# Two consecutive rows of one expert on each partition: another cut of the expert loads in a mixture-of-experts block

## The chip, the core and the metric

The kernel runs on one core of one Trainium2 chip. The metric is the device time of one execution in microseconds; lower is better. The core has a matrix engine (TensorE: PE, and PEld for its weight loads), VectorE (DVE), ScalarE (ACT), GpSimd (POOL) and SyncE (SP), which here issues nearly all DMAs, and 16 DMA engines that share each load.

## What is computed

A block of a small language model for 256 tokens of 1024 features, all in float32: a recurrent mixer and an attention mixer, gated and projected, then a layer norm, then 32 experts in 4 groups of 8, each token sent to two experts of its best group, then a second layer norm. The part that the change touches is the experts:

```python
x = layer_norm(DN_ALPHA * h + mixed, ln1_g[l], ln1_b[l])
ffn = hier_moe(x, ...)
# in hier_moe, for the tokens xb of an expert e:
gate, up = jnp.split(xb @ w_gate_up[e], 2, axis=-1)      # w_gate_up[e]: 1024 x 1024
y = (jax.nn.silu(gate) * up) @ w_down[e]                 # w_down[e]: 512 x 1024
x = layer_norm(DN_ALPHA * x + ffn, ln2_g[l], ln2_b[l])
```

A product sums over the rows of the expert's matrix, so these rows may be taken in any order as long as the features of the tokens stand in the same one.

## The kernel before

The first part (lines 191 to 1007) computes the two mixers, the first norm and the routing. Its weights pass through four places of 8 KB a partition (`W_PL`), each loaded as 512 rows of 512 columns.

The second part (from line 1146) takes the experts in 8 quads of 4 (`NQ`). The 24 loads of a quad (`NEXP`) are 1 MB each, numbered `i = 24 q + r`: r = 0 to 15 hold w_gate_up, r = 16 to 23 w_down. `e_source` (L124) gives the source: the 128 rows of the chunk k of two experts, each partition getting one row (4 KB) of either. So loads 2k and 2k + 1 bring the chunk k of the quad's four experts. Loads go to places in the order of `E_PL` (24 places, one of which becomes the accumulator); a place is used again 23 loads later. `e_tile` (L181) issues the loads in order of their number, all on SP; some are issued far ahead, in the first part, as its own buffers come free. Loads 8, 10 and half of 25 are issued as halves (`e_halves`, L131) into other buffers. In the last quad the down loads are cut by columns instead (L151 to L166): 512 columns of all four experts (r = 16 to 19), then 256 (20, 21), then 128 (22, 23).

For each quad, `gather` (L887) makes `xg`: for each k, a matmul whose weights are the 128 normed features `hx[:, t, k * P:(k + 1) * P]` and whose moving operand places up to 32 tokens of each expert; ScalarE and VectorE apply the norm's gain and bias (`g1_cols`, `b1_cols`, from the rows that are loaded at L205 and transposed at L394). Then `by_expert` (L1137) issues, for k = 0 to 7 and each half j of the columns, four matmuls, one for each expert on its own 32 columns of the array; each shows as two instructions. `act_T` (L1041) applies the activation, transposes the 128 x 512 result in four pieces (L1048) and `by_expert` multiplies by the down weights, k = 0 to 3. `combine` (L1056) adds the weighted result to the accumulator within the next quad, after its k = 1; the gather for the next quad stands after k = 4. In the last quad, down products, combine and the norm's statistics follow each other by column slices (L1191 to L1228), and then come the closing norm and the stores. Behind a condition that this input doesn't meet stands `overflow` (L1098).

Of the kernel before, what the change touches and what calls it, by code (L numbers as in the profile page):

```python
# [16 lines left out]
ALU = mybir.AluOpType  # L17
# [3 lines left out]
P = 128  # L21
# [39 lines left out]
def kernel(ctx: ExitStack, tc: tile.TileContext, x, w_in, b_in, rows_in, relb, w_proj_a, w_proj_b,  # L61
# [56 lines left out]
    def e_place(i):  # L118
# [2 lines left out]
        n = len(E_PL) - 1  # L121
        return E_PL[i] if i < n else (E_PL[:N_ACC] + E_PL[N_ACC + 1:])[(i - n) % n]

    def e_source(i):  # L124

        q, r = divmod(i, NEXP)
        src, k = (w_gate_up[0], r // 2) if r < 16 else (w_down[0], (r - 16) // 2)
        e0 = 4 * q + 2 * (r % 2)
        return src[e0:e0 + 2, k * P:(k + 1) * P, :].rearrange("e p c -> p e c")

    def e_halves(i, halves, ns=(0, 1)):  # L131

        ts = e_tiles.setdefault(i, [None] * 2)
        for n in ns:
            nc.sync.dma_start(halves[n], e_source(i)[:, n])
            ts[n] = halves[n]

    def e_get(i):
        q, r = divmod(i, NEXP)
        if i == E_SPL:  # L140
            e_halves(i, [part(n, "e_half") for n in (1, 2)])
            return
        if i == E_PART:
            p = place(E_PL[-1], "e_t")
            e_halves(i, (part(3, "e_half"), p[0]))
            e_halves(E_NEXT, (p[1],), (0,))
            return
        t = place(e_place(i), "e_t")
        if i == E_NEXT:
            e_halves(i, (None, t[0]), (1,))  # L150
        elif q == NQ - 1 and 16 <= r < 20:  # L151

            t = t[2].rearrange("p (e c) -> p e c", e=4)
            r0 = (r - 16) * P
            nc.sync.dma_start(t, w_down[0, 4 * q:4 * q + 4, r0:r0 + P, 0:512].rearrange("e p c -> p e c"))
            e_tiles[i] = [t[:, e, :] for e in range(4)]
        elif q == NQ - 1 and r >= 20:

            nk, w = (2, 256) if r < 22 else (4, 128)
            c0, k0 = (512, 2 * (r - 20)) if r < 22 else (768 + 128 * (r - 22), 0)  # L160
            t = t[2].rearrange("p (k e c) -> p k e c", k=nk, e=4)
            for k in range(nk):
                r0 = (k0 + k) * P
                nc.sync.dma_start(t[:, k], w_down[0, 4 * q:4 * q + 4, r0:r0 + P, c0:c0 + w].rearrange(
                    "e p c -> p e c"))
            e_tiles[i] = [[t[:, k, e, :] for e in range(4)] for k in range(nk)]  # L166
        else:
            t = t[2].rearrange("p (e c) -> p e c", e=2)
            nc.sync.dma_start(t, e_source(i))  # L169
            e_tiles[i] = [t[:, e, :] for e in range(2)]  # L170

    e_next = [0]

# [9 lines left out]
            e_load()  # L183
        return e_tiles[i]

    def e_rows(i, j):

        return [w[:, j * 512:(j + 1) * 512] for n in range(2) for w in e_tile(i + n)]


    xs = place(XS, "xs")[2].rearrange("p (t d) -> p t d", t=NT)
# [8 lines left out]
    run(wl[0])  # L200
    x_load(512, 1024)
    run(wl[1])
    NR = 88
    rows = const.tile([NR, P], F32, name="rows")
    nc.sync.dma_start(rows, rows_in)  # L205
    run(w_load())
# [195 lines left out]
        return cols[:, 32 + c // P:32 + c // P + n]  # L402

    g1_cols, b1_cols, ng_cols = cols[:, 0:8], cols[:, 8:16], cols[:, 84:88]
    lnr = rows[0:32]
    nb_f = const.tile([P, HG], F32, name="nb_f")
    nc.vector.tensor_scalar(nb_f, bias_cols(C_F, HG), -1.0, None, op0=ALU.mult)
# [479 lines left out]
    def gather(pos_of, idx, tl, groups=(range(0, 4), range(4, 8))):  # L887

        oh, xg = tl["oh"], tl["xg"]
        n = idx.shape[-1]  # L890
        j = P // n
        banks = [big1("px") for g in groups]

        def pick(b, k, t):
            g = groups[b]
            dst = banks[b][:, (k - g[0]) * P:(k - g[0] + 1) * P]
            nc.tensor.matmul(dst, hx[:, t, k * P:(k + 1) * P], oh[:, t, :], start=(k == g[0] and t == 0),  # L897
                             stop=(k == g[-1] and t == 1), skip_group_check=True)
            return dst

        def rows_of(t):
            return nc.vector.tensor_tensor(v3(oh[:, t, :], n), pos_of(t)[:, :, None].to_broadcast([P, j, n]),
                                           idx[:, None, :].to_broadcast([P, j, n]), op=ALU.is_equal)

        rows_of(0)
        yield
        for b in (0, 1):
            for k in groups[b]:
                pick(b, k, 0)
        rows_of(1)  # L910
        for b, g in enumerate(groups):
            if b == 1:
                for c in range(2, len(groups)):
                    for k in groups[c]:
                        pick(c, k, 0)
            for k, pk in [(k, pick(b, k, 1)) for k in g]:
                if k % 2:
                    xg_put[:] = [nc.vector.tensor_scalar(xg[:, k, :], pk, g1_cols[:, k:k + 1], b1_cols[:, k:k + 1],  # L918
                                                         op0=ALU.mult, op1=ALU.add)]
                else:  # L920
                    nc.scalar.activation(xg[:, k, :], pk, AF.Identity, bias=b1_cols[:, k:k + 1],  # L921
                                         scale=g1_cols[:, k:k + 1])
            yield

    def places_of(q, tl, **kw):
# [115 lines left out]
    def act_T(gu):  # L1041
        sg = y_tile()[:, 0:512]
        nc.scalar.activation(sg, gu[:, 0, :], AF.Sigmoid)  # L1043
        nc.vector.tensor_tensor(sg, gu[:, 0, :], sg, op=ALU.mult)  # L1044
        nc.vector.tensor_tensor(sg, gu[:, 1, :], sg, op=ALU.mult)
        ph = big1("ph")
        for k in range(4):
            nc.tensor.transpose(ph[:, k * P:(k + 1) * P], sg[:, k * P:(k + 1) * P], ident)  # L1048
        nc.scalar.activation(h_tile()[:, 0:512], ph, AF.Copy)

    def y_out(py):
# [46 lines left out]
    def overflow():  # L1098
# [4 lines left out]
        with tc.If(cmx > CAP):  # L1103
            with tc.For_i(0, NE) as e:
                ce = nc.values_load(cnt[0:1, bass.ds(e, 1)], min_val=0, max_val=S)
                for g in range(2):
                    with tc.If(ce > CAP + g * P):
# [8 lines left out]
                        for k in range(KD):  # L1116
                            for j in range(2):
                                w = y_tile()[:, j * 512:(j + 1) * 512]
                                nc.gpsimd.dma_start(w, w_gate_up[0, bass.ds(e, 1), k * P:(k + 1) * P,
                                                               j * 512:(j + 1) * 512].rearrange("e p c -> p (e c)"))  # L1120
                                nc.tensor.matmul(gu[:, j, :], xg[:, k, :], w, start=(k == 0), stop=(k == KD - 1))
                        act_T(gu)
# [2 lines left out]
                        for k in range(4):  # L1125
                            for j in range(2):
                                w = xw[:, j * 512:(j + 1) * 512]
                                nc.gpsimd.dma_start(w, w_down[0, bass.ds(e, 1), k * P:(k + 1) * P,
                                                            j * 512:(j + 1) * 512].rearrange("e p c -> p (e c)"))
                                nc.tensor.matmul(py[:, j, :], hT_of(k), w, start=(k == 0), stop=(k == 3))  # L1130
                        y_out(py)
# [15 lines left out]
    for q in range(NQ):  # L1147
# [7 lines left out]
        for k in range(KD):  # L1155
# [5 lines left out]
                with tc.issue_after(ins):  # L1161
                    run(feed)
            for j in range(2):
                ins = by_expert(gu[:, j, :], tl["xg"][:, k, :], e_rows(n0 + 2 * k, j), k == 0, k == KD - 1,
                                pin=q == 0 and j == 0)
            if k == 1 and pending:
                combine(wT_of(q - 1))
# [17 lines left out]
        if q < NQ - 1:  # L1185
            for k in range(4):
                for j in range(2):
                    by_expert(py[:, j, :], hT_of(k), e_rows(n0 + 16 + 2 * k, j), k == 0, k == 3)
            y_out(py)
            pending = True  # L1190
        else:  # L1191
# [85 lines left out]
def _layout(i):  # L1277
# [1 line left out]
    def r(n):  # L1279
        return np.asarray(i[n]).reshape(-1, P)  # L1280

    i["rows"] = np.concatenate([r(n) for n in ("ln1_g", "ln1_b", "ln2_g", "ln2_b", "b_in", "lb_logits", "hg_norm_g")])
    rel = np.concatenate([np.asarray(i["rel_bias"]), np.ones((1, MH), np.float32)])
    i["relb"] = np.concatenate([rel, _bucket_rows()], axis=1)
    wg, we = np.asarray(i["w_group"])[0], np.asarray(i["w_expert"])[0]
# [20 lines left out]
```

## Time and profile before

| | |
|---|---|
| median of 3 runs | 670.04 us (669.97 to 670.57) |
| the profiled execution | 670.6 us, its span 669.0 us |
| PE busy, PEld busy | 555.9 us (83%), 311.9 us (47%) |
| DVE, ACT, POOL busy | 229.3 us, 162.2 us, 9.2 us |
| DMA | 238.48 MB, 356 GB/s over the span |
| mean granted TensorE clock | 0.944 |

The span runs from the first to the last instruction of the profiled execution. A busy engine need not be the one that sets the time: matmuls are pipelined and waits for a load can lie within them. The page divides the span into 40 slices and gives for each the busy share of the engines, the granted clock and what the DMA moved; the chain follows the work that ended last back through what released it.

### The profile page before, as it was taken

The numbers are of one execution on the slowest core, as the hardware profiler recorded it, in microseconds if no ns is written. First come the engines' busy times: TensorE is split into PE (matmuls) and PEld (weight loads), VectorE is DVE, ScalarE is ACT, GpSimd is POOL, SyncE is SP. The second block draws the span as 40 slices with busy tenths as digits, with TensorE's granted clock in tenths as the row PEclk, the third lists the DMA queues.
The fourth block names the chain that finished last, engine by engine and source line by source line (L and its number), as shares of the span: only waits on it lengthen the run. The fifth ranks groups of instructions, "written<-read, shape, count | busy, mean of one in ns | idle before, by whom it ended". The sixth has DMA issues, their size and how long they took to land.

```text
span 669.0 us, 9743 instructions
## 1 busy us (share of the span) xinstructions
PE 555.9 (83%) x4018; PEld 311.9 (47%) x4019; DVE 229.3 (34%) x531; ACT 162.2 (24%) x321; POOL 9.2 (1%) x32
## 2 busy tenths in 40 slices
PE   8999999999998989897666865786776778677686
PEld 8989899999987543323111311131121113123124
DVE  4698668866577314220010002010201010020027
ACT  5653568955553200101000100010001001001010
POOL 1000000000000000000000000000000000000000
PEclk9999999999999979999899888897989888799979
DMA  8998676676997699999999999999999999999993
GB/s 306 380 373 310 193 252 201 237 286 207 334 389 263 252 409 408 409 411 408 408 410 409 409 409 409 408 409 410 408 410 409 410 409 409 409 410 408 403 340 125
DMA packets 78832, 238.48 MB, mean 356 GB/s; under 512 B 5182, under 2 KB 12991, under 8 KB 78783
## 3 DMA queue, kind: packets, MB, share of 16 engines
q1 hardware_dynamic: 78767, 237.80, 92.4%
q8 instruction: 33, 0.54, 0.3%
q14 instruction: 16, 0.13, 0.1%
q10 hardware_dynamic: 16, 0.01, 0.0%
HBM read 236.74 MB, written 1.06 MB: 355 GB/s over the span
## 4 chain that ended last, share of the span: by engine, by line
DMA 46%; PE 45%; DVE 3%; SPq 3%; ACT 2%; issue 1%; DVEq 0%; ACTq 0%
DMA e_t<-in_w_gate_up_dram 30%; PE psT L325 17%; DMA e_t<-in_w_down_dram 14%; PE gu L1141 8%; PE psN L332 7%; PE py L1141 4%; SPq L169 2%; PE px L897 2%; PE pr L1071 1%; PE pc L1061 1%; DMA xs<-in_x_dram 1%; PE pl L487 1%; PE pg L836 1%; PE pw L1205 1%; PE pom L672 0%
## 5 line engine op out<-in xcount | busy, mean ns | idle before, releaser
L1141 PE MATMUL gu<-e_t,xg 128*32 128x512 f32 x1012 | 166.8, 640 | 54.7 <-DMA e_t<-in_w_gate_up_dram 50.4
L1141 PEld LDWEIGHTS gu<-e_t,xg 128*32 128x32 f32 x1012 | 35.2, 113 | 165.3 <-DMA e_t<-in_w_gate_up_dram 94.6
L1141 PE MATMUL py<-e_t,hw 128*32 128x512 f32 x480 | 87.3, 744 | 25.1 <-DMA e_t<-in_w_down_dram 20.3
L282 DVE TENSOR_TENSOR w_spl<-w_t,w_spl 128x512 fp32r<-128x512 f32 x120 | 82.1, 689 | 44.5 <-ACT w_spl L281 43.6
L281 ACT ACTIVATE w_spl<-w_t 128x512 fp32r<-128x512 f32 x120 | 75.1, 631 | 71.6 <-PE psT L325 45.0
L325 PE MATMUL psT<-xT_hi,w_spl 128*128 128x256 f32 x576 | 86.2, 287 | 0.7 <-ACT w_spl L281 0.6
L325 PEld LDWEIGHTS psT<-xT_hi,w_spl 128*128 128x128 f32 x576 | 75.6, 192 | 3.9 <-ACT w_spl L281 2.3
L918 DVE TENSOR_SCALAR xg<-px,cols 128x128 f32<-128x128 f32 x32 | 12.6, 409 | 134.1 <-ACT xg L921 131.8
L1141 PEld LDWEIGHTS py<-e_t,hw 128*32 128x32 f32 x480 | 17.8, 126 | 86.8 <-DMA e_t<-in_w_down_dram 46.4
L921 ACT ACTIVATE xg<-px,cols 128x128 f32<-128x128 f32 x32 | 13.9, 456 | 175.0 <-PE px L897 169.8
L325 PE MATMUL psT<-xT_lo,w_spl 128*128 128x256 f32 x288 | 46.2, 283 | 0.0
L1054 DVE COPY yb<-py 128x512 f32<-128x512 f32 x7 | 4.8, 691 | 107.8 <-ACT yb L1053 107.8
L325 PEld LDWEIGHTS psT<-xT_lo,w_spl 128*128 128x128 f32 x288 | 39.6, 191 | 0.0
L1044 DVE TENSOR_TENSOR yb<-gu,yb 128x512 f32<-128x512 f32 x8 | 5.5, 691 | 91.5 <-ACT yb L1043 91.5
L1061 PE MATMUL pc<-yb,hw 128*128 128x512 f32 (+2 forms) x72 | 31.8, 568 | 5.2 <-ACT yb L1053 4.2
L897 PEld LDWEIGHTS px<-oh,hx 128*128 128x128 f32 x256 | 29.4, 192 | 9.5 <-issue 9.5
L1062 DVE TENSOR_TENSOR acc<-acc,pc 128x512 f32<-128x512 f32 (+2 forms) x36 | 22.4, 627 | 28.8 <-PE pc L1061 28.8
L897 PE MATMUL px<-oh,hx 128*128 128x128 f32 x256 | 31.0, 279 | 0.0
L1053 ACT ACTIVATE yb<-py 128x512 f32<-128x512 f32 x7 | 4.2, 597 | 96.0 <-PE py L1141 96.0
L1043 ACT ACTIVATE yb<-gu 128x512 f32<-128x512 f32 x8 | 4.8, 598 | 80.9 <-PE gu L1141 80.9
L1061 PEld LDWEIGHTS pc<-yb,hw 128*128 128x128 f32 x72 | 12.0, 189 | 25.2 <-ACT yb L1053 9.7
L332 PE MATMUL psN<-w_spl,mix 128*128 128x512 f32 (+1 forms) x105 | 23.3, 376 | 0.1
(235 smaller groups left out, 463.4 us busy)
## 6 DMA issues: line engine op xcount, KB each, us to landing
e_t<-in_w_gate_up_dram SPq DMA_DIRECT2D x125, 1024.0 KB, 18.4
e_t<-in_w_down_dram SPq DMA_DIRECT2D x60, 1024.0 KB, 18.4
w_t<-in_w_in_dram SPq DMA_DIRECT2D x20, 1024.0 KB, 7.2
w_t<-in_w_out_dram SPq DMA_DIRECT2D x4, 1024.0 KB, 7.1
w_t<-in_w_proj_a_dram SPq DMA_DIRECT2D x2, 1024.0 KB, 5.1
w_t<-in_w_proj_b_dram SPq DMA_DIRECT2D x2, 1024.0 KB, 5.1
e_t<-in_w_down_dram SPq DMA_DIRECT2D x4, 512.0 KB, 12.2
e_t<-in_w_down_dram SPq DMA_DIRECT2D x8, 256.0 KB, 5.2
```

Of the source, the lines that this page charges most:

```text
L169: nc.sync.dma_start(t, e_source(i))
L281: ins = [nc.scalar.activation(hi, w, AF.Copy), nc.vector.tensor_tensor(lo, w, hi.bitcast(F32), op=ALU.subtract)]
L282: nc.vector.tensor_tensor(lo, w, hi.bitcast(F32), op=ALU.subtract)]
L325: nc.tensor.matmul(ps[:, c, :], a[:, c * P:(c + 1) * P], b[k], start=(k == 0 and n == 0 and c % 2 == 0), stop=(k == nk - 1 and n == 2 and ...
L332: nc.tensor.matmul(ps, a[k][:, tsl], b, start=(k == 0 and n == 0), stop=(k == nk - 1 and n == 2), skip_group_check=skip)
L487: nc.tensor.matmul(pl[j * 32:(j + 1) * 32, i, :], kf[:, c:c + 32], qx[:, c:c + 32], start=True, stop=True, skip_group_check=True)
L897: nc.tensor.matmul(dst, hx[:, t, k * P:(k + 1) * P], oh[:, t, :], start=(k == g[0] and t == 0), stop=(k == g[-1] and t == 1), skip_group_c ...
L918: xg_put[:] = [nc.vector.tensor_scalar(xg[:, k, :], pk, g1_cols[:, k:k + 1], b1_cols[:, k:k + 1], op0=ALU.mult, op1=ALU.add)]
L921: nc.scalar.activation(xg[:, k, :], pk, AF.Identity, bias=b1_cols[:, k:k + 1], scale=g1_cols[:, k:k + 1])
L1061: nc.tensor.matmul(pc, wT[:, t * P:(t + 1) * P], y_tile()[:, sl], start=True, stop=True)
L1062: nc.vector.tensor_tensor(acc[t][:, sl], acc[t][:, sl], pc, op=ALU.add)
L1141: ins = nc.tensor.matmul(dst[sl], xT[:, sl], ws[e], start=first, stop=last, skip_group_check=True)
```

## The change

Each full expert load takes 256 rows of one expert instead of 128 rows of two. Partition p gets the rows 2p and 2p + 1, which lie next to each other in HBM (8 KB) and next to each other in the place. Loads 4b to 4b + 3 then bring the chunks 2b and 2b + 1 of the quad's four experts, and the chunk k is the rows 256 (k // 2) + k % 2 in steps of 2 (`part_of`). So that the features fit, the gather's weights are taken in steps of 2, the norm's gain and bias are loaded once more in that order (16 more rows), and the activation's transposes take every second column. The last quad's column-cut loads and the overflow's loads take the same rows. The core of the diff:

```diff
+    def part_of(k):
+        c = 256 * (k // 2) + k % 2
+        return slice(c, c + 255, 2)
     def e_source(i):
         q, r = divmod(i, NEXP)
-        src, k = (w_gate_up[0], r // 2) if r < 16 else (w_down[0], (r - 16) // 2)
-        e0 = 4 * q + 2 * (r % 2)
-        return src[e0:e0 + 2, k * P:(k + 1) * P, :].rearrange("e p c -> p e c")
+        src, b = (w_gate_up[0], r // 4) if r < 16 else (w_down[0], (r - 16) // 4)
+        return src[4 * q + r % 4, 256 * b:256 * b + 256, :].rearrange("(p s) c -> p (s c)", s=2)
...
-            nc.sync.dma_start(halves[n], e_source(i)[:, n])
+            nc.sync.dma_start(halves[n], e_source(i)[:, n * 1024:(n + 1) * 1024])
...
-            r0 = (r - 16) * P
-            nc.sync.dma_start(t, w_down[0, 4 * q:4 * q + 4, r0:r0 + P, 0:512].rearrange("e p c -> p e c"))
+            nc.sync.dma_start(t, w_down[0, 4 * q:4 * q + 4, part_of(r - 16), 0:512].rearrange("e p c -> p e c"))
...
-            t = t[2].rearrange("p (e c) -> p e c", e=2)
-            nc.sync.dma_start(t, e_source(i))
-            e_tiles[i] = [t[:, e, :] for e in range(2)]
+            nc.sync.dma_start(t[2], e_source(i))
+            e_tiles[i] = t[0:2]
...
-    def e_rows(i, j):
-        return [w[:, j * 512:(j + 1) * 512] for n in range(2) for w in e_tile(i + n)]
+    def e_rows(i, k, j):
+        return [e_tile(i + 4 * (k // 2) + e)[k % 2][:, j * 512:(j + 1) * 512] for e in range(4)]
...
-    NR = 88
+    NR = 104
...
+    g1_parts, b1_parts = cols[:, 88:96], cols[:, 96:104]
...
-            nc.tensor.matmul(dst, hx[:, t, k * P:(k + 1) * P], oh[:, t, :], start=(k == g[0] and t == 0),
+            nc.tensor.matmul(dst, hx[:, t, part_of(k)], oh[:, t, :], start=(k == g[0] and t == 0),
...
-            nc.tensor.transpose(ph[:, k * P:(k + 1) * P], sg[:, k * P:(k + 1) * P], ident)
+            nc.tensor.transpose(ph[:, k * P:(k + 1) * P], sg[:, part_of(k)], ident)
...
-                ins = by_expert(gu[:, j, :], tl["xg"][:, k, :], e_rows(n0 + 2 * k, j), k == 0, k == KD - 1,
+                ins = by_expert(gu[:, j, :], tl["xg"][:, k, :], e_rows(n0, k, j), k == 0, k == KD - 1,
...
-                    by_expert(py[:, j, :], hT_of(k), e_rows(n0 + 16 + 2 * k, j), k == 0, k == 3)
+                    by_expert(py[:, j, :], hT_of(k), e_rows(n0 + 16, k, j), k == 0, k == 3)
```

## Rows read from the trace of the kernel before

**Rows 1.** Page: clock and DMA in 40 slices; the chain's shares by engine.

```profile
PEclk9999999999999979999899888897989888799979
GB/s 306 380 373 310 193 252 201 237 286 207 334 389 263 252 409 408 409 411 408 408 410 409 409 409 409 408 409 410 408 410 409 410 409 409 409 410 408 403 340 125
DMA 46%; PE 45%; DVE 3%; SPq 3%; ACT 2%; issue 1%; DVEq 0%; ACTq 0%
```

**Rows 2.** Stages: busy us and instructions of each engine; last three columns clock, DMA, GB/s.

```profile
core 0: us, PE busy (x) PEld busy (x) DVE busy (x) ACT busy (x) POOL busy (x), PEclk, DMA share, GB/s
225.00:230.00 5.00, 5.00 (x48) 2.27 (x41) 0.00 (x0) 0.00 (x0) 0.00 (x0) 1.00 0.88 344
230.00:630.00 400.00, 303.32 (x1757) 96.99 (x1757) 52.93 (x100) 29.69 (x61) 5.59 (x14) 0.91 1.03 409
464.30:467.30 3.00, 2.88 (x14) 0.75 (x16) 0.00 (x0) 0.00 (x0) 0.00 (x0) 0.50 1.02 408
634.00:657.00 23.00, 19.00 (x157) 7.46 (x160) 8.07 (x25) 2.45 (x5) 0.00 (x0) 0.85 0.98 318
640.00:645.00 5.00, 4.90 (x12) 1.38 (x12) 0.00 (x0) 0.05 (x1) 0.00 (x0) 0.50 1.06 363
```

**Rows 3.** The chain in order of time: start us, us, what; four of its links.

```profile
286.25 18.14 DMA e_t<-in_w_gate_up_dram
304.44 1.94 PE gu L1141 x12
...
615.90 18.17 DMA e_t<-in_w_gate_up_dram
...
652.32 4.50 DMA e_t<-in_w_down_dram
```

**Rows 4.** DMA packets: 300:600 us with its queue's MB and share; 631:639; 642:646.

```profile
DMA packets 31787, 122.72 MB, mean 409 GB/s; under 512 B 1869, under 2 KB 1869, under 8 KB 31768
q1 hardware_dynamic: 31768, 122.47, 102.3%
...
DMA packets 1492, 3.10 MB, mean 388 GB/s; under 512 B 47, under 2 KB 47, under 8 KB 1491
...
DMA packets 1305, 1.40 MB, mean 351 GB/s; under 512 B 42, under 2 KB 1199, under 8 KB 1305
```

**Rows 5.** DMA queue of instruction fetches, packets, MB, share: 37.1:37.8 us; 383:384 us.

```profile
q14 instruction: 2, 0.02, 5.5%
...
q14 instruction: 1, 0.01, 2.0%
```

**Rows 6.** Timeline of PE: start, us, what; 218, 461 to 468, 634 us.

```profile
218.92 3.64 PE L1141 MATMUL gu<-e_t,xg 128*32 128x512 f32 x32
...
461.86 1.05 PE L1141 MATMUL py<-e_t,hw 128*32 128x512 f32 x4 [0.65 <-DMA e_t<-in_w_down_dram]
464.42 3.88 PE L1141 MATMUL py<-e_t,hw 128*32 128x512 f32 x16 [1.51 <-DMA e_t<-in_w_down_dram]
...
634.12 1.91 PE L1141 MATMUL gu<-e_t,xg 128*32 128x512 f32 x12 [1.53 <-DMA e_t<-in_w_gate_up_dram]
```

**Rows 7.** Timeline of weight loads ahead of the first quad.

```profile
215.81 2.98 PEld L897 LDWEIGHTS px<-oh,hx 128*128 128x128 f32 x26
```

**Rows 8.** The line L523: duration ns min/median/max, first and last start.

```profile
L523 DVE TENSOR_TENSOR h<-h,h x7: 677/681/685, 45.3 to 78.4; 128x512 f32<-128x512 f32 x7
```

**Rows 9.** DMA of 205:225 us in 40 slices of 0.5 us.

```profile
GB/s 246 360 434 426 426 90 0 0 66 172 385 393 401 410 328 262 401 344 377 377 295 385 336 148 57 49 49 8 0 0 0 33 0 49 229 360 320 98 147 139
```

**Rows 10.** Timeline of SP's issues around the first quad.

```profile
221.29 28.61 SPq L169 DMA_DIRECT2D e_t<-in_w_gate_up_dram  x14
```

**Rows 11.** Timeline of PE in the last quad's end.

```profile
638.33 1.09 PE L1048 MATMUL ph<-ident,yb 128*128 128x128 f32 x4 [2.30 <-DVE yb L1045]
...
656.87 0.43 PE L1141 MATMUL py_c<-e_t,hw 128*32 128x128 f32 x8 [0.29 <-DMA e_t<-in_w_down_dram]
```

More of the change, by code (lines that the diff above doesn't have):

```diff
@@ L162, in e_get @@
             for k in range(nk):
-                r0 = (k0 + k) * P
-                nc.sync.dma_start(t[:, k], w_down[0, 4 * q:4 * q + 4, r0:r0 + P, c0:c0 + w].rearrange(
+                nc.sync.dma_start(t[:, k], w_down[0, 4 * q:4 * q + 4, part_of(k0 + k), c0:c0 + w].rearrange(
                     "e p c -> p e c"))
@@ L917, in gather @@
                 if k % 2:
-                    xg_put[:] = [nc.vector.tensor_scalar(xg[:, k, :], pk, g1_cols[:, k:k + 1], b1_cols[:, k:k + 1],
-                                                         op0=ALU.mult, op1=ALU.add)]
-                else:
-                    nc.scalar.activation(xg[:, k, :], pk, AF.Identity, bias=b1_cols[:, k:k + 1],
-                                         scale=g1_cols[:, k:k + 1])
+                    xg_put[:] = [nc.vector.tensor_scalar(xg[:, k, :], pk, g1_parts[:, k:k + 1],
+                                                         b1_parts[:, k:k + 1], op0=ALU.mult, op1=ALU.add)]
+                else:
+                    nc.scalar.activation(xg[:, k, :], pk, AF.Identity, bias=b1_parts[:, k:k + 1],
+                                         scale=g1_parts[:, k:k + 1])
             yield
@@ L1118, in overflow @@
                                 w = y_tile()[:, j * 512:(j + 1) * 512]
[L1119 removed]
+                                nc.gpsimd.dma_start(w, w_gate_up[0, bass.ds(e, 1), part_of(k),
                                                                j * 512:(j + 1) * 512].rearrange("e p c -> p (e c)"))
@@ L1127, in overflow @@
                                 w = xw[:, j * 512:(j + 1) * 512]
-                                nc.gpsimd.dma_start(w, w_down[0, bass.ds(e, 1), k * P:(k + 1) * P,
+                                nc.gpsimd.dma_start(w, w_down[0, bass.ds(e, 1), part_of(k),
                                                             j * 512:(j + 1) * 512].rearrange("e p c -> p (e c)"))
@@ L1280, in r @@
         return np.asarray(i[n]).reshape(-1, P)
-    i["rows"] = np.concatenate([r(n) for n in ("ln1_g", "ln1_b", "ln2_g", "ln2_b", "b_in", "lb_logits", "hg_norm_g")])
+    i["rows"] = np.concatenate([r(n) for n in ("ln1_g", "ln1_b", "ln2_g", "ln2_b", "b_in", "lb_logits", "hg_norm_g")]
+                               + [r(n).reshape(4, P, 2).transpose(0, 2, 1).reshape(8, P)
+                                  for n in ("ln1_g", "ln1_b")])
     rel = np.concatenate([np.asarray(i["rel_bias"]), np.ones((1, MH), np.float32)])
```

## The prediction, made before the change was run

> **What bounds the kernel now.** I read the page's slices and chain first, then the stages, then the chain in order of time, then the DMA by stretch. The slices [rows 1] show two kernels in one: up to slice 13 (counted from 0) the DMA moves 190 to 390 GB/s and the chain runs through the engines; from slice 14 (234 us) it stands at 408 to 411 GB/s until slice 36, and the chain is 46% DMA. The stages say the same [rows 2]: from 230 to 630 us the 16 DMA engines are busy 1.03 of the time (packets overlap a little) at 409 GB/s, while PE, with 303 us "busy" out of 400, waits. The chain [rows 3] shows how: a load takes 18.14 us from issue to landing because the queue ahead of it is full, PE computes 1.94 us on it as soon as it lands, and the next such link follows. So in this stretch only bytes per microsecond count, and an engine's work counts only where it follows the last landing: at the end of the last quad, when the gate/up weights have landed (634.07 us in the chain, from 615.90 plus 18.17) and the activation, the down products and the closing norm remain.
>
> **The change, part by part.**
>
> *The packets.* From 300 to 600 us q1 shows 31768 packets, 1869 of them under 512 B (completions), and 122.47 MB: 4096 B a packet [rows 4]. That is one row of one expert. After the change a partition takes two rows that are neighbours in HBM and in SBUF, so a load of 1 MB is 128 pieces of 8 KB where it was 256 of 4 KB. What a piece costs follows from three stretches in which the engines never rest: at 4 KB 409 GB/s, at 2 KB 388 GB/s (631 to 639 us), at 1 KB 351 GB/s (642 to 646 us, a few 2 KB pieces among them) [rows 4]. Per engine that is 16 x 4096 B / 409 = 160.2 ns, 16 x 2048 / 388 = 84.5 ns and 16 x 1024 / 351 = 46.7 ns: 75.7 ns for 2 KB more, 37.8 ns for 1 KB more, hence a fixed 8.8 ns and 27.05 B/ns. An 8 KB piece then costs 160.2 + 2 x 75.7 = 311.6 ns, which is 421 GB/s. The trace holds real 8 KB pieces, instruction fetches on q14: two in 0.7 us take 5.5% of 16 engines, 0.7 x 16 x 0.055 / 2 = 308 ns; one amid the saturated stretch takes 2.0% of 1 us, 320 ns [rows 5]. So the bounds are 308 ns (425.6 GB/s) and 320 ns (409.6, no gain; this one shares its engine with q1's pieces, which an expert's load would not). I take 311.6, which is nearest to the undisturbed fetch and comes from this queue's own loads. Saved over the 400 us of saturation: 400 x (1 - 409/421) = 11.4 us; by the bounds 0.6 to 15.6. The last quad's down loads keep 2 KB, 1 KB and 512 B pieces; they only skip every second row, for which I take nothing, and at 318 GB/s over 23 us [rows 2] 3% of them would be 0.7 us either way.
>
> The fixed share is where the Trainium skill differs. The page "DMA: Bandwidth & Descriptors", section "Why small descriptors are slow (HBM only)", gives about 3 cycles a packet beside one cycle for each 32 B. By that 4 KB is 131 beats and 8 KB 259, and only 1.15% would be saved. The fit above has over twice that fixed cost. I hold to the fit; the page's result is a rival below.
>
> *The order of loads and waits.* The number and order of SP's issues stay, none passes another queue, and no wait is added to another engine. But four loads (four experts, two k) now become free together, after the second k, where two became free after each k. The kernel has 23 places; about 7 loads are in flight (18.14 us at 2.56 us a load), some 15 landed or in use. Holding two or three longer leaves over ten, which hides it once PE waits for landings. Where PE starts late it is bare: in q = 0 DMA all but stands still from 217 us [rows 9] until PE frees the first places; SP's run of full loads starts at 221.29 [rows 10]. After the change the first release comes after k = 1, about 222.5 (32 matmul instructions from 218.92, 3.64 us [rows 6]), but four places at once: DMA restarts 1.5 us later and then at full rate. Moved until 230 before: about 0.65 MB up to 225 (the last six slices of [rows 9] at 0.5 us each) and 5 us x 344 GB/s = 1.7 MB [rows 2], 2.4 in all; after, some 6 us x 421 = 2.5 MB. I take 0, with bounds of -1.5 and +1.5 us.
>
> *PE's burst after a landing.* Before, the last landing of a quad's gate/up leaves 6 of 8 matmuls, 12 instructions, 1.91 us [rows 6]. After, tile e = 3 lands last and has been waited for in k = 6, j = 0: left are 1 + 4 + 8 = 13 matmuls, 26 instructions. At the full clock (32 in 3.64 us) that is 3.0 us; at 1.2 GHz (16 in 3.88 us after a burst of 4 and a wait [rows 6], granted 0.50 there [rows 2]) 6.3 us. Between landings PE now has 2 instructions and a wait of over 2 us, three times over, so the slow row is the nearer. As the clock came back after the slow 640 to 645 us (0.50) for the rest of 634 to 657 (0.85 in all) [rows 2], part of the burst may run fast, and I take 5.2 us: +3.3. In the earlier quads this is hidden by the next landings (4 x 2.49 us a group). In the last quad it is on the path: everything from there to the end is PE, ACT and DVE work in a row, and the final weights (the chain's last load, issued at 652.32, landing 4.50 us later [rows 3]) made PE wait only 0.29 us [rows 11]. So +3.3 - 0.3 = +3.0 us, bounds +0.8 and +4.1.
>
> The clock is the other rule against this change: the Trainium skill, "TensorE: Matmul & The Clock Gate", section "Loop structure matters more than you think", warns of a wait for a DMA between bunches of matmuls, after which the engine is cold. The row agrees (16 in 3.88 us after a wait); by it the whole burst would be slow and the sum 1.1 us worse.
>
> *Strided operands.* The gather's weights (L897) and the transposes read every second element. The 26 weight loads ahead of q = 0 take 2.98 us [rows 7]; if each took double it would be +3.0 us on the path, and later gathers would be hidden. The nearest stride in the trace is VectorE's L523, whose seven runs go from neighbours to 64 apart and all take 677 to 685 ns [rows 8]. I take 0. The second set of gains, 16 more rows of 512 B, moves 8 KB, 0.02 us at 409 GB/s, beside w_in loads.
>
> *Sum.* 670.6 (the profiled execution: span 669.0 and 1.6 around it) - 11.4 + 0 + 3.0 + 0 = 662.2. The median of the runs is 0.56 lower than the profiled one, 670.04: 661.6.
>
> **The rivals.**
> - *No better rate, and the burst is paid* (slower). If the limit in the stretch is bytes, or the loads are still cut into 4 KB, the -11.4 is gone and 670.0 + 3.0 = 673.0. For it: the 8 KB fetch at 320 ns among q1's pieces [rows 5], and that nothing in the trace moves 8 KB into SBUF. Against: the rate falls steadily with the piece, 409, 388, 351, so the piece counts. It decides where the saving equals 3.0 us, at 412 GB/s, 318 ns for 8 KB.
> - *A smaller fixed cost.* If only 1.15% is saved, as the page's rule has it: 400 x 0.0115 = 4.6, so 670.0 - 4.6 + 3.0 = 668.4, on the edge of what counts as faster.
> - *Strided weights cost double.* q = 0 starts 3.0 us later, the transposes of the last quad (1.09 us [rows 11]) another 1: 665.6.
> - *PE falls behind.* A quad holds 192 expert instructions: 46.6 us at 16 in 3.88, and with gather, combine and activation over 60, more than the 59.8 us that DMA would need. But PE that never waits is not slow (32 in 3.64 us makes 21.8), so this can't last; at worst a late start of q = 1 and 2 eats the gain: about 671.
>
> **How the numbers follow.** Forecast 0.70, no better rate 0.14, smaller fixed cost 0.08, strided weights 0.04, PE behind 0.04. The forecast's own bounds: 421 GB/s against 425.6 (-4.2), the burst from +0.8 to +4.1, the start of q = 0 by 1.5 either way: taken together about 656.5 to 666. The range goes on to 668.8 to take in the smaller fixed cost and the strides; no better rate lies outside. About 0.2% (1.3 us) is what a measurement of this kernel can tell from no change: faster 0.70 + 0.04 + half of 0.08 + 0.01 = 0.79; same 0.06; slower 0.15.
>
> **What would show it.** Packets of 8192 B in 230 to 620 us and over 418 GB/s there confirm the first step; 409 with 8 KB packets makes bytes the limit. The last gate/up landing should come near 623 us. The matmuls after it should number 26 and take 3 to 6.3 us, and the granted clock in the expert stretch should fall below 0.91. L897's weight loads should stay at 192 ns. DMA idle after 224 us, or PE without a DMA wait before the last quad's end, would make me wrong on the order of waits; a final PE wait for DMA of more than 0.3 us would mean that the burst wasn't on the path.

## The result: 1.64% less time, and the profile after

| | before | after |
|---|---|---|
| median of 4 runs beside each other | 670.31 us (669.97 to 674.21) | 660.36 us (659.15 to 662.23) |
| ratio, 95% interval | | 0.9836 (0.9817 to 0.9855) |
| the profiled execution, its span | 670.6 us, 669.0 us | 660.4 us, 658.8 us |

The forecast was 661.6 us (656.5 to 668.8). Its number is close, but two of its terms were wrong in opposite directions: the burst (+3.0 us) was not paid, and a later start (+1.46 us), which the sum did not have, came in. The profile of after shows it.

First the page (clock and DMA in 40 slices, the chain by engine) and the packets from 300 to 600 us with their queue:

```profile
PEclk9999999999999898989979889887998798899899
GB/s 298 383 381 314 210 256 193 210 286 211 329 386 280 191 423 421 422 420 420 421 421 422 420 419 421 417 420 422 420 422 420 422 420 422 420 421 421 410 343 120
DMA 50%; PE 43%; DVE 3%; ACT 2%; issue 1%; SPq 1%; DVEq 0%; ACTq 0%
...
DMA packets 17317, 126.21 MB, mean 421 GB/s; under 512 B 1923, under 2 KB 1923, under 8 KB 1923
q1 hardware_dynamic: 17297, 125.95, 101.0%
```

From slice 14 on the DMA moves 421 GB/s where it moved 409 [rows 1, 4]. Of q1's packets all but the 1923 small ones are 8 KB: 125.95 MB / 15374 is 8192 B. The cost of a piece is 16 x 8192 / 421 = 311.3 ns; the fit gave 311.6.

The start of the first quad, on PE, its weight loads and SP (start us, us, what), and the clock there (columns as in [rows 2]):

```profile
215.17 0.38 PE L860 MATMUL pp<-sel,oh 128*128 128x32 f32 x2 [1.66 <-DVE sel L857]
...
215.61 4.84 PE L901 MATMUL px<-oh,hx 128*128 128x128 f32 x26
220.38 3.64 PE L1145 MATMUL gu<-e_t,xg 128*32 128x512 f32 x32
224.03 0.33 SPq L141 DMA_DIRECT2D e_t<-in_w_gate_up_dram  x1
...
L901 PEld LDWEIGHTS px<-oh,hx x256: 193/196/332, 215.6 to 559.5; 128*128 128x128 f32 x128
...
217.00:220.00 3.00, 3.00 (x16) 3.00 (x16) 0.00 (x0) 0.46 (x1) 0.00 (x0) 0.50 0.00 1
225.00:230.00 5.00, 5.00 (x48) 1.31 (x41) 0.78 (x3) 0.46 (x1) 0.40 (x1) 1.00 0.99 387
230.00:630.00 400.00, 313.48 (x1788) 108.48 (x1784) 53.90 (x102) 29.94 (x62) 5.58 (x14) 0.91 1.01 420
```

The gather's 26 weight loads are the same work as in [rows 7]. In the kernel before, PE spent 3.15 us on the gather:

```profile
215.84 3.15 PE L897 MATMUL px<-oh,hx 128*128 128x128 f32 x26
```

After, it spends 4.84 us, with a granted clock of 0.50 from 217 to 220 us. The experts begin at 220.38 instead of 218.92 [rows 6], SP's first release comes at 224.03 instead of 221.29 [rows 10].

The end: two links of the chain, the timeline of PE after the last gate/up landing, and the clock there:

```profile
603.24 19.85 DMA e_t<-in_w_gate_up_dram
641.51 5.14 DMA e_t<-in_w_down_dram
...
623.14 5.12 PE L1145 MATMUL gu<-e_t,xg 128*32 128x512 f32 x26 [1.47 <-DMA e_t<-in_w_gate_up_dram]
630.55 0.71 PE L1052 MATMUL ph<-ident,yb 128*128 128x128 f32 x4 [2.29 <-DVE yb L1049]
631.95 1.92 PE L1145 MATMUL py<-e_t,hw 128*32 128x512 f32 x16 [0.69 <-ACT hw L1053]
633.80 1.98 PE L1209 MATMUL pw<-ln,ident 128*128 128x512 f32 x4
635.72 1.92 PE L1145 MATMUL py<-e_t,hw 128*32 128x512 f32 x16
...
645.93 0.43 PE L1145 MATMUL py_c<-e_t,hw 128*32 128x128 f32 x8 [0.22 <-DMA e_t<-in_w_down_dram]
646.69 0.43 PE L1145 MATMUL py_c<-e_t,hw 128*32 128x128 f32 x8 [0.34 <-DMA e_t<-in_w_down_dram]
...
623.00:626.00 3.00, 2.86 (x16) 0.79 (x20) 0.00 (x0) 0.00 (x0) 0.00 (x0) 0.50 1.05 388
626.00:647.00 21.00, 16.81 (x162) 6.73 (x154) 8.07 (x25) 2.45 (x5) 0.00 (x0) 1.00 1.00 311
```

The last gate/up load lands at 623.09, the burst is 26 instructions in 5.12 us. Yet PE still waits for the last down weights, 0.22 and 0.34 us. The same stretch in the kernel before, the lines that [rows 11] left out:

```profile
640.10 1.93 PE L1141 MATMUL py<-e_t,hw 128*32 128x512 f32 x8 [0.69 <-ACT hw L1049]
641.96 3.50 PE L1205 MATMUL pw<-ln,ident 128*128 128x512 f32 x4
645.39 2.78 PE L1141 MATMUL py<-e_t,hw 128*32 128x512 f32 x24
```

There the half clock came later, from 640 to 645 us [rows 2]. From the transposes to the last down product of 512 columns PE worked 1.09 + 1.93 + 3.50 + 2.78 = 9.30 us; after, 0.71 + 1.92 + 1.98 + 1.92 = 6.53. The burst took 3.21 us more and the work behind it 2.77 less.

Three marks divide a profiled execution: the start of the first expert matmuls (S), the start of the last down products (E), and the end of the span.

| | S | E | E - S | span - E | span |
|---|---|---|---|---|---|
| before | 218.92 | 656.87 | 437.95 | 12.1 | 669.0 |
| after | 220.38 | 646.69 | 426.31 | 12.1 | 658.8 |
| order_4k | 220.69 | 658.41 | 437.72 | 12.1 | 670.5 |
| plain_reads | 220.55 | 646.72 | 426.17 | 12.2 | 658.9 |
| warm_gather | 218.90 | 645.14 | 426.24 | 12.2 | 657.3 |
| warm_gather_b | 219.46 | 645.77 | 426.31 | 12.1 | 657.9 |
| before_warm | 218.66 | 656.86 | 438.20 | 12.1 | 669.0 |
| last_by_pairs | 218.74 | 645.49 | 426.75 | 12.1 | 657.6 |
| pw_late_warm | 219.22 | 645.64 | 426.42 | 12.2 | 657.8 |

So the 10.2 us of span are -11.64 in the stream and +1.46 at its start. Of the -11.64, -12.44 lie ahead of the last gate/up landing (634.07 before, 623.09 after) and +0.80 behind it. Those 0.80 us are not the burst: from that landing to E the 16 DMA engines are busy 0.99 of the time before and 1.02 after, and they move 7.65 MB where they moved 7.29, so more of the stream was left at the landing.

The trace's chain goes back from the last load (641.51) over SP's issues and a combine to the burst, as if the burst had held up the last issues. But the place of that load was last read by the first two chunks of the same quad, done by 602 us, and the DMA engines had no idle time that an earlier issue could have filled.

### The profile page after: what moved, and what is told of

Its sections match the earlier page's. It is cut to its first block, busy times and chain, and to the rows that moved or that the text cites. A ratio compares the mean times of both kernels' runs of the same rounds, so it can differ in the third digit from the quotient of the medians.

```text
span 658.8 us, 9739 instructions
## 1 busy us (share of the span) xinstructions
PE 558.9 (85%) x4018; PEld 321.8 (49%) x4019; DVE 229.3 (35%) x531; ACT 161.8 (25%) x321; POOL 9.2 (1%) x32
## 4 chain that ended last, share of the span: by engine, by line
DMA 50%; PE 43%; DVE 3%; ACT 2%; issue 1%; SPq 1%; DVEq 0%; ACTq 0%
DMA e_t<-in_w_gate_up_dram 33%; PE psT L328 17%; DMA e_t<-in_w_down_dram 16%; PE psN L335 7%; PE gu L1145 6%; PE py L1145 3%; PE px L901 3%; DMA xs<-in_x_dram 1%; PE pr L1075 1%; PE pc L1065 1%; PE pl L491 1%; PE pg L840 1%; PE pom L676 0%; PE pw L656 0%; PE ph L1052 0%
## 5 line engine op out<-in xcount | busy, mean ns | idle before, releaser
L1145 PE MATMUL gu<-e_t,xg 128*32 128x512 f32 x1012 | 172.5, 632 | 44.1 <-DMA e_t<-in_w_gate_up_dram 39.8
L1145 PEld LDWEIGHTS gu<-e_t,xg 128*32 128x32 f32 x1012 | 40.2, 114 | 155.1 <-DMA e_t<-in_w_gate_up_dram 77.0
L1145 PEld LDWEIGHTS py<-e_t,hw 128*32 128x32 f32 x480 | 19.6, 132 | 81.1 <-issue 39.2
L901 PEld LDWEIGHTS px<-oh,hx 128*128 128x128 f32 x256 | 33.5, 211 | 7.5 <-issue 7.5
L901 PE MATMUL px<-oh,hx 128*128 128x128 f32 x256 | 35.1, 300 | 0.0
L1052 PE MATMUL ph<-ident,yb 128*128 128x128 f32 x32 | 6.3, 323 | 17.9 <-DVE yb L1049 17.9
```

The lines of the kernel that those rows point to most:

```text
L901: nc.tensor.matmul(dst, hx[:, t, part_of(k)], oh[:, t, :], start=(k == g[0] and t == 0), stop=(k == g[-1] and t == 1), skip_group_check=True)
L1145: ins = nc.tensor.matmul(dst[sl], xT[:, sl], ws[e], start=first, stop=last, skip_group_check=True)
```

## Experiments

### Only the order of the loads: order_4k

```diff
     def part_of(k):
-        c = 256 * (k // 2) + k % 2
-        return slice(c, c + 255, 2)
+        return slice(k * P, (k + 1) * P)
...
-        return src[4 * q + r % 4, 256 * b:256 * b + 256, :].rearrange("(p s) c -> p (s c)", s=2)
+        return src[4 * q + r % 4, 256 * b:256 * b + 256, :].rearrange("(s p) c -> p s c", s=2)
...
```

> The loads in the changed kernel's order (256 rows of one expert each, so four experts become free together and the last landing leaves 26 matmul instructions), but partition p takes the rows p and p + 128, so the pieces are 4 KB as before and the features stand in their plain order, with no strided operand. Theory (the gain is the piece's size; the order costs about a microsecond): 409 GB/s from 300 to 600 us, time 670.3 + about 1 = 671, between 670 and 673; against the changed kernel +11. The gather ahead of the first quad takes 3.0 us as before. Rival 1 (the order of loads, by one expert at a time, is what brought the gain, for instance because reads stay in one matrix): about 661 with 4 KB pieces. Rival 2 (the prediction's burst of +3 us lies on the path in full): 673 to 674.

Measured: 671.3 us (670.06 to 672.11), 0.9999 (0.9986 to 1.0012) of the kernel before. Its packets from 300 to 600 us, its first gather, its burst, the first products behind it and its last down products:

```profile
DMA packets 31777, 122.68 MB, mean 409 GB/s; under 512 B 1869, under 2 KB 1869, under 8 KB 31758
...
215.98 4.78 PE L900 MATMUL px<-oh,hx 128*128 128x128 f32 x26
...
635.06 3.62 PE L1144 MATMUL gu<-e_t,xg 128*32 128x512 f32 x26 [1.51 <-DMA e_t<-in_w_gate_up_dram]
642.29 1.92 PE L1144 MATMUL py<-e_t,hw 128*32 128x512 f32 x16 [0.69 <-ACT hw L1052]
...
658.41 0.43 PE L1144 MATMUL py_c<-e_t,hw 128*32 128x128 f32 x8 [0.33 <-DMA e_t<-in_w_down_dram]
```

With 4 KB pieces the rate is 409 again and the whole gain is gone: it is the piece. The new order, four places at a time and 26 instructions after the last landing, costs nothing that can be measured: E - S is 437.72 against 437.95. The expectation missed one thing: the gather took 4.78 us here too, without any strided operand.

### The strides alone: plain_reads

```diff
-            nc.tensor.matmul(dst, hx[:, t, part_of(k)], oh[:, t, :], start=(k == g[0] and t == 0),
+            nc.tensor.matmul(dst, hx[:, t, k * P:(k + 1) * P], oh[:, t, :], start=(k == g[0] and t == 0),
...
-            nc.tensor.transpose(ph[:, k * P:(k + 1) * P], sg[:, part_of(k)], ident)
+            nc.tensor.transpose(ph[:, k * P:(k + 1) * P], sg[:, k * P:(k + 1) * P], ident)
```

> The changed kernel, but the gather's weights and the activation's transposes read neighbouring elements instead of every second one; the features then stand in the wrong order for the rows of the weights, so the experts' products are of other pairs, of the same size. Theory (the stride costs about 0.01 us a weight load, and the first gather's extra 1.7 us is the half clock that it met): the first gather shrinks by 0.2 us at the same clock and by up to 1.7 us if the clock stays up, time 0 to 1.0 us below the changed kernel, 659.5 to 660.5. Rival (the stride itself slows the first gather by 1.7 us): the 26 instructions take 3.0 us at any clock, and the time is 1.5 us lower, about 658.9.

Measured: 660.13 us (659.05 to 660.42), 0.9833 (0.9816 to 0.985), the same as the changed kernel. The first gather on PE, and all gather weight loads (ns min/median/max):

```profile
215.84 4.78 PE L901 MATMUL px<-oh,hx 128*128 128x128 f32 x26
...
L901 PEld LDWEIGHTS px<-oh,hx x256: 186/192/338, 215.8 to 561.0; 128*128 128x128 f32 x128
```

The slow gather stays without the strides. In the gather they cost 196 - 192 = 4 ns a weight load. In the activation's transposes they cost more: the median weight load takes 209 ns in the changed kernel and 140 here. The four transposes of the last quad take 0.71 us with strides and 0.63 in order_4k, and the time of the whole kernel shows neither.

### The clock at the first gather: warm_gather, warm_gather_b, before_warm

```diff
-N_WARM = (6, 1, 1, 5, 0, 14, 4)
+N_WARM = (6, 1, 1, 5, 0, 14, 10)
```

> The changed kernel with six more matmuls on the identity before the second routing step, which fill PE's idle 1.66 us at 213.5. Theory (the first gather met a half clock after that idle time, from 216.6 to 220.0): the granted clock stays at 1.0 through the gather, which takes 3.2 us instead of 4.8, the first expert matmuls start 1.6 us earlier and so does the DMA stream: 658.8. Rival (the clock falls whatever PE did there, or the stride is what costs): no change, 660.4; or 0.3 us slower, if the added matmuls delay the routing.

> warm_gather once more, beside the next three on one chip, since they are to be told from it by tenths of a per cent. Both theories: 0.9825 of the kernel before within 0.002, some 659.2; first expert matmul near 218.8, the last down weights 426.2 us after it.

> The kernel before with the six added matmuls of warm_gather. Theory (which level of the clock the first gather meets after PE's idle 1.66 us is chance, in the kernel before as much as in the changed one): the runs lie closer together than those of the kernel before (669.06 to 673.77), near its lowest, 669.3 to 670.3, and the distance to warm_gather (659.2) is what the loads alone bring, 10.5 to 11.5 us. Rival (only the changed kernel's strided gather meets the half clock): the median stays at 670.9, as the kernel before beside it, with the same scatter.

Measured: warm_gather 659.2 us (658.86 to 659.38), 0.9825 (0.9809 to 0.9841); again 659.4 us, 0.9817 (0.98 to 0.9833); before_warm 669.41 us (667.9 to 671.15), 0.9969 (0.9956 to 0.9982). warm_gather's gather, first expert matmuls, burst, the first products behind it and last down products, and its clock from 217 to 220 us:

```profile
215.66 3.31 PE L901 MATMUL px<-oh,hx 128*128 128x128 f32 x26
218.90 3.64 PE L1145 MATMUL gu<-e_t,xg 128*32 128x512 f32 x32
621.50 3.62 PE L1145 MATMUL gu<-e_t,xg 128*32 128x512 f32 x26 [1.45 <-DMA e_t<-in_w_gate_up_dram]
628.82 3.62 PE L1145 MATMUL py<-e_t,hw 128*32 128x512 f32 x16 [0.69 <-ACT hw L1053]
645.14 0.43 PE L1145 MATMUL py_c<-e_t,hw 128*32 128x128 f32 x8 [0.36 <-DMA e_t<-in_w_down_dram]
...
217.00:220.00 3.00, 3.00 (x29) 2.20 (x32) 0.46 (x2) 0.92 (x2) 0.00 (x0) 1.00 0.00 1
```

At the full clock the gather takes 3.31 us with strides against 3.15 without, so the strides are 0.16 us and the clock 1.5. Of the profiled executions shown in this text, six have no filler in PE's idle 1.66 us ahead of the gather, and three of them met the half clock there (after, order_4k, plain_reads), three not (before, last_by_pairs, tail_rows_warm); all eight with the filler had the full clock. By these counts chance alone would give such a split about once in 18, so the filler's effect is likely and not certain. The strided gather isn't the cause, since order_4k and plain_reads have the plain one; that the kernel before can meet the half clock too is likely, but no profile shows it. For the changed kernel the filler gave 659.2 and 659.4 instead of 660.36, as expected, but the intervals of the ratios overlap. before_warm came out at the expected median; that its runs would lie closer together was wrong, they spread over 3.3 us, and its distance to warm_gather is 10.2 us, a little under the expected 10.5 to 11.5. Its own profile (span 669.0, E - S 438.20) is as long as that of the kernel before, so what its faster executions saved stays open.

### The burst: last_by_pairs and late_pe_warm

The last four gate/up loads of the last quad as one chunk of two experts each, with 4 KB pieces:

```diff
+        if q == NQ - 1 and 12 <= r < 16:
+            e0 = 4 * q + 2 * (r % 2)
+            return w_gate_up[0, e0:e0 + 2, part_of(r // 2), :].rearrange("e p c -> p e c")
...
```

> The changed kernel, but in the last quad the four loads of the last two chunks of the gate/up weights are cut as before: one chunk of two experts each, with 4 KB pieces, of the same rows. After the last landing 12 matmul instructions are left instead of 26. Theory (the end is set by the stream of the last down weights, so the burst is covered): the last gate/up product ends 1 to 3 us earlier relative to the landing, PE then waits 1.5 to 3 us longer for the last weights, and the time is 0.3 us longer for four loads of 2.56 instead of 2.49 us: 660.4 to 660.8. Rival (the prediction: the burst of +3 us is on the path): 657.5 to 658.

Measured: 659.84 us (659.19 to 661.41), 0.9842 (0.9823 to 0.9861), no change. PE:

```profile
621.68 1.91 PE L1151 MATMUL gu<-e_t,xg 128*32 128x512 f32 x12 [1.51 <-DMA e_t<-in_w_gate_up_dram]
...
641.94 0.43 PE L1151 MATMUL py_c<-e_t,hw 128*32 128x128 f32 x8 [0.46 <-DMA e_t<-in_w_down_dram]
642.93 0.43 PE L1151 MATMUL py_c<-e_t,hw 128*32 128x128 f32 x8 [0.57 <-DMA e_t<-in_w_down_dram]
...
645.49 0.42 PE L1151 MATMUL py_c<-e_t,hw 128*32 128x128 f32 x8 [0.50 <-DMA e_t<-in_w_down_dram]
```

The burst is 12 instructions and 1.91 us again, and what PE gains it waits out at the down weights, of which three waits are shown. E - S is 426.75, 0.4 us longer, as the theory had it. The median is 0.6 us under the expected 660.4; the profiled execution met the full clock at the first gather (S 218.74).

The other way round, four matmuls ahead of the last eight gate/up matmuls:

```diff
+            if q == NQ - 1 and k == KD - 1:
+                pz = big1("pz")
+                for _ in range(4):
+                    tc.keep_in_program_order(nc.tensor.matmul(pz, ident, ..., start=True, stop=True))
```

> warm_gather with four matmuls of 128 x 512 on the identity ahead of the last eight gate/up matmuls of the last quad, after the last landing: 3.9 us more PE work there at the full clock (the combine's matmuls of that shape take 0.98 us each), more where the clock is at half. Theory (PE's chain from the last gate/up landing and the stream of the down weights end within half a microsecond of each other, so a longer burst is paid as soon as that margin is used up): 3.3 us and more over warm_gather, 662.5 to 664.5, and PE no longer waits for the last down weights. Rival (the stream has several microseconds of cover): under 1 us longer, 659.2 to 660.

Measured: 661.33 us (660.14 to 662.24), 0.9848 (0.983 to 0.9865). PE:

```profile
623.21 3.70 PE L1170 MATMUL pz<-xg,ident 128*128 128x512 f32 x8
...
632.49 2.78 PE L1145 MATMUL py<-e_t,hw 128*32 128x512 f32 x24 [0.69 <-ACT hw L1053]
...
646.09 0.86 PE L1145 MATMUL py_c<-e_t,hw 128*32 128x128 f32 x24
```

The span is 1.4 us longer than warm_gather's (658.7 against 657.3), between the theory's 3.3 and the rival's 1. The ratio to the kernel before is 0.0023 higher, some 1.5 us, with intervals that overlap, and the medians are 2.1 us apart. PE no longer waits for the last weights (no wait in the last row), so its chain is the longer one now. But of the 3.70 us added only 1.4 are paid in the profiled executions: the down products run at the full clock here, 24 in 2.78 us, where warm_gather has 16 in 3.62. As between before and after, a longer burst was followed by faster work. It isn't a rule: in order_4k the burst of 26 (3.62 us) and the 16 products behind it (1.92 us) both ran at the full clock.

### The end of the stream: pw_late_warm, tail_rows_warm, tail_pairs_warm, tail_both_warm

The bias's matmuls moved behind the last combine:

```diff
-    pw2 = big2("pw2")
-    for j in range(2):
-        nc.tensor.matmul(pw2[:, j, :], ident, lb2[:, j * 512:(j + 1) * 512], start=True, stop=False)
...
+    pw2 = big2("pw2")
+    for j in range(2):
+        tc.keep_in_program_order(nc.tensor.matmul(pw2[:, j, :], ident, ..., start=True, stop=False))
     keep_warm(N_WARM[5], ident)
```

> warm_gather, but the two matmuls that add the second norm's bias (1.98 us of PE at the full clock) stand behind the last combine, in place of eight of the filler matmuls there, and no longer between the down products. PE's chain from the last gate/up landing to the last down product gets 2 to 3.8 us shorter, the stream stays as it is. Theory (the stream's end binds): PE waits some 2 us longer for the last weights and the time falls by 0.4 us at most, 658.8 to 659.4. Rival (PE's chain binds): 657 to 657.5.

The last quad's down loads cut by full rows first:

```diff
-        elif q == NQ - 1 and 16 <= r < 20:
+        elif q == NQ - 1 and 20 <= r < 22:
-            nc.sync.dma_start(t, w_down[0, 4 * q:4 * q + 4, part_of(r - 16), 0:512]...)
+            nc.sync.dma_start(t, w_down[0, 4 * q:4 * q + 4, part_of(r - 18), 0:512]...)
...
             for k in range(2):
-                by_expert(py[:, 0, :], hT_of(k), e_tile(n0 + 16 + k), k == 0, k == 3)
+                for j in range(2):
+                    by_expert(py[:, j, :], hT_of(k), e_rows(n0 + 16, k, j), k == 0, False)
```

> The changed kernel with the last quad's down loads cut otherwise: the first four are 256 full rows of one expert (8 KB pieces), two then take 512 columns of the other half of the rows (2 KB), one 256 columns (1 KB) and one twice 128 columns (512 B); the products of the first 256 rows are made ahead for all columns. 4 MB move at 421 instead of 388 GB/s and half as many small pieces follow: by the rates of the changed kernel's last 24 us (388, 351, 285 GB/s) the stream ends 1.5 us earlier. Theory (stream and PE chain end together): PE's chain binds and only 0.3 to 0.5 us come out, 659.6 to 660.1 beside the changed kernel's 660.4. Rival 1 (the stream alone sets the end): 1.5 us, 658.9. Rival 2 (PE's chain alone): no change.

(Despite its label this one has no filler ahead of the gather.) The other two put the edits together; in tail_both_warm the column slices have PSUM tiles of their own:

> warm_gather with both edits of the last quad: the cut of its down loads by full rows first, and its last four gate/up loads as one chunk of two experts (12 matmul instructions after the last landing). Theory (two ends that bind together): the stream ends 1.5 - 0.3 us earlier and PE's chain 1.7 us or more, so 1.0 to 1.4 us come out where each edit alone gave 0.5 or less: 657.8 to 658.2 against 659.2. Rival (one of the two alone binds): the time of one edit alone, 658.7 to 659.2.

> pw_late_warm with the last quad's down loads cut by full rows first as in tail_rows_warm, the column slices' products on PSUM tiles of their own. There the stream alone was shortened and PE's chain ended last (no wait for the last weights, landing to last product 25 us); here both are shorter. Theory (stream and PE's chain end together, so only both edits at once bring anything): the last down product starts 423.8 to 424.8 us after the first expert matmul instead of 426.2, 657.0 to 658.0. Rival (something else holds the end, SP's issues or ScalarE's copies): no change, 659.2, or slower.

| | median us | ratio to before | E - S |
|---|---|---|---|
| pw_late_warm | 660.08 | 0.9825 (0.9808 to 0.9841) | 426.42 |
| tail_rows_warm | 662.08 | 0.9841 (0.9819 to 0.9863) | 428.98 |
| tail_pairs_warm | 660.51 | 0.9838 (0.9821 to 0.9855) | 427.29 |
| tail_both_warm | 660.11 | 0.9822 (0.9805 to 0.9839) | 429.8 |

(tail_both_warm's E is taken from its chain, 648.92 for the last six instructions; its profiled execution was its slowest, 662.98 of 659.31 to 662.98.) PE of pw_late_warm, then of tail_rows_warm, then the DMA of the changed kernel and of tail_rows_warm from 622 us on in slices of 1 us:

```profile
629.21 5.34 PE L1145 MATMUL py<-e_t,hw 128*32 128x512 f32 x32 [0.69 <-ACT hw L1053]
645.64 0.42 PE L1145 MATMUL py_c<-e_t,hw 128*32 128x128 f32 x8 [0.46 <-DMA e_t<-in_w_down_dram]
...
640.99 0.64 PE L1146 MATMUL py<-e_t,hw 128*32 128x256 f32 x8 [0.70 <-ACT yb L1219]
647.86 0.42 PE L1146 MATMUL py<-e_t,hw 128*32 128x128 f32 x8
...
GB/s 367 389 387 387 395 375 385 387 380 375 369 352 350 346 333 318 314 254 280 282 298 292 272 165 4 0 0 0 0 0 0 0 209 387 377 76 0 0 0 0
...
GB/s 401 442 410 434 410 408 420 389 385 401 393 362 379 366 337 324 254 240 258 271 92 20 2 0 0 0 16 0 0 0 0 0 0 76 383 377 213 0 0 0
```

With PE's chain alone made shorter the stream sets the end and nothing comes out (E - S 426.42). With the stream alone made shorter (it is over some 2 us earlier) the last product starts later, waits for no weights, and PE has waited for ScalarE's copies instead (0.70 us, 0.50 and 0.40 behind it), probably because slices and copies share a PSUM tile (argued, not tried alone). So neither edit alone ends the kernel sooner, and what the shorter stream is worth isn't shown, since its edit lengthened PE's chain. What I expected of both together, 1 to 2 us, did not come. The clock of tail_both_warm where it lost the time:

```profile
632.00:636.00 4.00, 4.00 (x19) 1.35 (x16) 0.00 (x0) 0.00 (x0) 0.00 (x0) 0.50 1.06 378
```

In that execution the burst took 5.96 us (granted clock 0.60), PE began the down products at half clock, and its chain was the longer by over 3 us. Whether a chain that keeps the full clock would bring the 2 us isn't settled. None of these four beats warm_gather.

### The fit at another size: pieces_2k_warm

```diff
-            nc.sync.dma_start(t[2], e_source(i))
+            t4 = t[2].rearrange("p (j s c) -> p j s c", j=2, s=2)
+            s4 = e_source(i).rearrange("p (s j c) -> p j s c", j=2, s=2)
+            for j in range(2):
+                nc.sync.dma_start(t4[:, j], s4[:, j])
...
```

> warm_gather, each full expert load as two of 512 KB, one for each half of the columns, so that the pieces are 2 KB; rows, operands and their order stay. Theory (a fixed 8.8 ns a piece and 27.05 B/ns, as fitted before the change): 84.5 ns a piece, 388 GB/s from 300 to 600 us, the stretch of 400 us at 421 GB/s becomes 434, time 693 (690 to 696). Rival (the fixed share is smaller, 3 cycles on 64, as the Trainium skill's page on DMA bandwidth has it, and 421 against 409 GB/s came from elsewhere): under 10 us longer, below 669.

Measured: 697.03 us (695.27 to 698.31), 1.0371 (1.035 to 1.0392).

```profile
DMA packets 60038, 115.95 MB, mean 386 GB/s; under 512 B 3531, under 2 KB 3531, under 8 KB 60019
q1 hardware_dynamic: 60019, 115.70, 104.9%
```

16 x 2048 / 386 = 84.9 ns a piece, the fit gave 84.5. The time lies 1 us above the expected range. The 400 us at 421 GB/s become 436 at 386, and the end is longer too, since the last gate/up load landed at 657.2 and the last products came 27 us later, over 3 more than in the changed kernel. The Trainium skill, "DMA: Bandwidth & Descriptors", section "Why small descriptors are slow (HBM only)", gives about 3 cycles a packet beside one for each 32 B. An estimate by it, 67 beats of which 64 carry data against 259 and 256, is 421 x 0.9664 = 407 GB/s and a loss of 14 us (my expectation's "under 10" was too small for it). The measured 386 speaks against it.

## Why the prediction was right, and where it was not

- *What bounds the kernel.* Right. The gain is the stream's, and span - E is 12.1 us in both.
- *The packets, -11.4.* Right: 8192 B, 421 GB/s, 311.3 ns. E - S fell by 11.64, and order_4k takes all of it back with the same order of loads. The fetch at 320 ns amid other pieces, the bound at which nothing would be gained, was no guide; the undisturbed one at 308 was nearer.
- *The order of loads and waits, 0.* Right: four places come free at once and DMA moves 387 GB/s from 225 to 230 us where it moved 344, and E - S of order_4k is that of the kernel before. The idle time after 224 us that I named as a sign against me did show, up to the release, but it came from the later start of the gather.
- *The start.* A term that the sum did not have. The 1.46 us by which the first quad starts later are the granted clock of 0.50 from 217 to 220 us, which three of six profiled executions without filler met and none of eight with it. I had the clock in the burst and did not look at PE's idle 1.66 us ahead of the gather, where the kernel before happened to keep the full clock.
- *The burst, +3.0.* The size was right (26 instructions, 5.12 us, taken as 5.2), the place was not. The step that failed is "in the last quad it is on the path": I read from a final wait of 0.29 us that 0.3 was all the cover. That wait told how far apart two chains ended in one execution, and PE's chain was not of fixed length. In after, the work behind the longer burst ran at 1.00 instead of 0.50 for part of the way, 2.77 us less, and the down weights still ended last. The stream of the last weights sets the end, and its DMA engines are busy without a break up to E. A burst of 12 instructions brings nothing (last_by_pairs), a chain 2 us shorter nothing (pw_late_warm), and of 3.7 us more 1.4 are paid (late_pe_warm). At the full clock the burst takes 3.62 us (order_4k, warm_gather) and not the 3.0 that I had scaled from 32 instructions in 3.64. The sign that I had named, a final wait of more than 0.3 us, stood in the trace: 0.22 and 0.34.
- *The clock.* The Trainium skill, "TensorE: Matmul & The Clock Gate", section "Loop structure matters more than you think", warns of a long wait for a DMA between matmuls, after which PE goes cold. Taken for the wait of 1.47 us here, as in the prediction, that would make the whole burst cold, and the rows differ: part of it ran at 0.50 in after (3.0 of its 5.12 us), none of it in warm_gather (26 in 3.62 us behind a wait of 1.45). The mean clock of the expert stretch stayed at 0.91 instead of falling.
- *The strides, 0.* Right for the time: 0.16 us on the first gather and 0.08 on the last quad's transposes. But a weight load did get slower, by 4 ns in the gather, where I had expected 192 ns to stay, and from 140 to 209 in the transposes.
- *The rivals.* No better rate: fell, by the 421 GB/s and by order_4k. A smaller fixed cost: fell, by 421 and by 386. Strides at double cost: fell, by plain_reads. PE behind: fell, since between 230 and 623 us PE waits 44 times for weights to land, 55.9 us in all.

Summed anew for the profiled executions: 670.6 - 11.64 + 1.46 = 660.4. The forecast for it was 662.2: 3.0 too much for the burst, 1.5 too little for the start, 0.2 for the stream. That the missing start took back half of the burst's error is luck.

## What to carry to other kernels

Where the 16 DMA engines never rest, count pieces: fit a fixed cost and a rate from stretches with different sizes in the same trace, and the fit carries to a size that the trace hardly shows (here to 8 KB within 0.3 ns; at 2 KB it held within 0.4 over a whole stream). A short wait at the end of a chain is the distance between two chains and no measure of what a longer one would cost; divide the span by marks (start of the stream, its end, the rest) and see which of them an edit moves. Work that runs after an idle stretch of PE can cost up to twice as much in some executions and not in others (16 down products 1.92 and 3.62 us), so one profile isn't enough to price it.

## What was unexpected of the hardware

- The clock that a short gather meets after 1.66 us of idle PE differs between executions of nearly the same program: 26 weight loads and matmuls take 3.15 to 3.31 us at 1.00 and 4.78 to 4.84 with 0.50 granted.
- A longer piece of work in the end of the kernel need not cost its length: 3.70 us of matmuls more made the span 1.4 us longer. Where the half clock falls there differs between runs with the same burst: into it (5.12 us in after, 5.07 in plain_reads), behind it (warm_gather and warm_gather_b, both 3.62 for the 16 down products) or into neither (order_4k). What decides it stays open.
- SP is held in the issue of some loads much longer than in that of others. The issues of the loads of the gate/up weights (ns min/median/max): 1 MB in order_4k, 1 MB in the changed kernel, 512 KB in pieces_2k_warm:

```profile
L171 SPq DMA_DIRECT2D e_t<-in_w_gate_up_dram x125: 367/2310/3202, 18.1 to 616.6; - x125
...
L172 SPq DMA_DIRECT2D e_t<-in_w_gate_up_dram x125: 327/328/1307, 17.7 to 603.2; - x125
...
L175 SPq DMA_DIRECT2D e_t<-in_w_gate_up_dram x250: 539/642/1745, 18.1 to 647.7; - x125
```

With 256 pieces of 4 KB the median issue takes 2.31 us, about the time of a load, and with 128 pieces of 8 KB 0.33 us. The number of pieces alone doesn't do it: 256 pieces of 2 KB take 0.64 us, in a stream as full as the others. What holds SP stays open. The shorter issue was no gain here, since the stream was full either way.
